# Extra, unread TensorE products behind two token searches and inside a norm, and three weight splits moved from GpSimd to VectorE

## The chip, the core and the metric

The kernel runs on one core of one Trainium2 chip. TensorE (PE) multiplies matrices, VectorE (DVE), ScalarE (ACT) and GpSimd (POOL) work elementwise, SyncE (SP) issues the transfers (DMA). Each engine has its own queue and works through it in order; engines meet at semaphores. The metric is the device time of one execution, in microseconds (us).

## What is computed

Two blocks run one behind the other over 512 tokens of 1024 features. The second has two layers, and what matters lies there: each layer ends with a mixture of 16 experts in which every expert chooses its 64 best tokens, and layer 1 begins with a norm. Cut from the reference:

```python
def modulate_2(x, g, shift, scale):
    return rmsnorm(x, g) * (1 + scale) + shift

def ec_moe(h, w_router, w_gate, w_up, w_down):
    b, n, d = h.shape
    cap = EC_CAPACITY_FACTOR * n // N_EXPERTS            # 64
    aff = jax.nn.softmax(h.astype(jnp.float32) @ w_router.astype(jnp.float32), axis=-1)
    g, idx = lax.top_k(aff.swapaxes(1, 2), cap)
    xs = jax.vmap(lambda hb, ib: hb[ib])(h, idx)
    a = jax.nn.silu(jnp.einsum('becd,edf->becf', xs, w_gate)) * jnp.einsum('becd,edf->becf', xs, w_up)
    y = jnp.einsum('becf,efd->becd', a, w_down) * g[..., None].astype(h.dtype)
    ...

    for l in range(DEPTH_2):                             # second_block, 2 layers
        h = modulate_2(x, norm_mix[l], sh_m, sc_m)
        ...                                              # layer 0: attention, layer 1: odd_mixer
        x = x + g_m * y
        x = x + g_f * ec_moe(modulate_2(x, norm_ffn[l], sh_f, sc_f), ...)
```

## The kernel before

X holds the residual with features on partitions (8 tiles f of 128 features, 512 tokens). Dense products are made in three passes, with each operand split into a high and a low part (`mm3`, line 453): `pieces` (line 437) takes a weight page, copies the high part `wh` on ScalarE (L447) and subtracts it for the low part `wl` (L448), on VectorE as a rule.

**The experts.** `moe` runs 8 rounds of two experts. Each round gathers the chosen tokens (`gather_part`, L1427: the normed tokens `xn` times a one-hot matrix `o`), and then multiplies with the gate, up and down weights (`product`, L1473), 24 MB a round, as transfers fill the buffers that TensorE gives free.

**The search.** `route_half` (line 1275) works on one half of the tokens. After the scores it copies them to `at` (L1307) and runs 8 rounds of `max`, `match_replace` and `max_index` on VectorE (L1314 to L1317). The second half (t0 = 256) runs last; what the first half found is merged with it in `best`. Between the two come `token_major` (line 1374), 32 transposes of X on TensorE (L1386) whose 8 banks ScalarE copies to `xn` (L1390), in layer 1 to `xt` also (L1393). The gather needs both `best` and all of `xn`.

**The norm of layer 1.** `down_last` ends layer 0's last round. It adds the experts' output to X for the first 256 tokens (`combine`, L1534 and L1537), calls `layer1_norm` (line 1593) for them, and does the same for the second 256. `norm_mod` sums the squares (L356, L344), takes the inverse root in small VectorE steps (`rsqrt`, L380 to L382), spreads it over partitions (`spread`, L397), and `norm_apply` makes 8 tiles of normed input (L432, L408, L409). Then the first product of the layer runs over the two halves of the tokens (`dense_f`, 192 products of 256 columns; each result is copied by L1611). Its four weight splits go to GpSimd (`lo`).

The order on each engine comes from a scheduler in the framework: an instruction goes into its engine's queue when the model takes it to be ready, and the queue then is fixed.

```python
        if t0 == 0:
            self.pcs = self.pieces(self.cw, 0, nc.gpsimd)
            self.cw = [next(self.pcs) for _ in range(3)]
```

## Time and profile before

| what | us |
|---|---|
| median of 3 runs | 2106.47 |
| lowest and highest run | 2102.52, 2106.98 |
| profiled execution, whole | 2108.61 |
| its span | 2106.8 |
| TensorE busy | 2003.3 (95%) |
| VectorE busy | 1007.3 (48%) |
| ScalarE busy | 559.0 (27%) |
| GpSimd busy | 17.2 (1%) |

The span is cut into 40 slices of 52.7 us on the profile's page. Transfers run at about 421 GB/s in slices 19 to 24 and 32 to 38, in the expert rounds of the two layers, and far below in most others. [...]

### The profile page before, as it was taken

What the parts mean: (1) busy time and instruction counts of PE and PEld (TensorE: products, weight loads), DVE (VectorE), ACT (ScalarE), POOL (GpSimd) and SP (SyncE); (2) the same over time, 40 slices, a digit from 0 to 9 for tenths busy, and PEclk for the clock granted to TensorE, in tenths of its full rate; (3) what the DMA queues carried; (4) which work ended last, traced back from release to release, by engine and by line L of the source; (5) the groups of instructions that cost most, each with busy time, mean ns of one, the idle gap of its engine ahead of it and who ended that gap; (6) DMA issues with size and microseconds to landing.
All of it is one profiled execution on the core that took longest, in us unless ns stands there. A gap on an engine that the chain in (4) does not pass through costs nothing. (4 is left out here: it accounts for less than half of the span.)

```text
span 2106.8 us, 26895 instructions
## 1 busy us (share of the span) xinstructions
PE 2003.3 (95%) x10922; PEld 1341.0 (64%) x10922; DVE 1007.3 (48%) x2004; ACT 559.0 (27%) x1039; POOL 17.2 (1%) x20
## 2 busy tenths in 40 slices
PE   7999999999999989989999999979998999999997
PEld 5759888788888978865444434428887544444442
DVE  4888995887584569661222212225457122222221
ACT  3344624243343359620000000023234000000000
POOL 0000000000000000000000000010000000000000
PEclk9999999999999999989999999989999999999999
DMA  9826484688411254449999999992254899999998
GB/s 362 288 80 231 172 296 160 222 289 244 144 48 41 79 159 114 174 160 374 408 421 421 421 421 421 420 363 81 100 193 161 328 409 422 422 422 422 422 422 327
DMA packets 158955, 582.84 MB, mean 277 GB/s; under 512 B 12593, under 2 KB 21713, under 8 KB 111984
## 3 DMA queue, kind: packets, MB, share of 16 engines
q1 hardware_dynamic: 158352, 580.70, 72.1%
q8 instruction: 86, 1.41, 0.3%
q10 hardware_dynamic: 288, 0.39, 0.1%
q14 instruction: 37, 0.30, 0.0%
q0 software_dynamic: 192, 0.03, 0.0%
HBM read 571.50 MB, written 2.11 MB: 272 GB/s over the span
## 5 line engine op out<-in xcount | busy, mean ns | idle before, releaser
L453 PE MATMUL mm<-b,wh 128*128 128x512 f32 (+1 forms) x2272 | 578.4, 344 | 1.3 <-ACT b L408 0.9
L453 PEld LDWEIGHTS mm<-b,wh 128*128 128x128 f32 x2272 | 394.9, 191 | 61.5 <-issue 6.7
L453 PE MATMUL mm<-b,wl 128*128 128x512 f32 (+1 forms) x1136 | 388.9, 344 | 0.8 <-DVE wl L448 0.8
L1473 PE MATMUL mm<-w,xs 128*64 128x512 f32 x1152 | 262.8, 600 | 12.6 <-DMA w<-w_u 12.6
L448 DVE TENSOR_TENSOR wl<-w,wh 128x1024 fp32r<-128x1024 f32 x160 | 194.0, 1222 | 160.6 <-ACT wh L447 159.4
L447 ACT CAST wh<-w 128x1024 fp32r<-128x1024 f32 x164 | 170.4, 1049 | 316.9 <-PE mm L453 276.3
L453 PEld LDWEIGHTS mm<-b,wl 128*128 128x128 f32 x1136 | 216.2, 191 | 27.9 <-issue 2.5
L1491 DVE TENSOR_TENSOR ea<-mm,ea 128x512 f32<-128x512 f32 x32 | 22.1, 692 | 398.0 <-PE mm L1473 374.6
L1473 PEld LDWEIGHTS mm<-w,xs 128*64 128x64 f32 x1152 | 84.9, 138 | 175.2 <-issue 141.4
L249 DVE SCALAR_TENSOR_TENSOR w<-w,sc 128x512 f32<-128x512 f32 x252 | 184.6, 748 | 3.8
L453 PE MATMUL mm<-wh,b 128*128 128x512 f32 (+1 forms) x640 | 179.1, 363 | 1.0 <-ACT b L408 1.0
L1473 PE MATMUL mm<-b,xs 128*64 128x512 f32 x720 | 166.1, 594 | 4.6 <-DMA b<-w_u 4.5
L1427 PEld LDWEIGHTS sm<-o,b 128*128 128x128 f32 x1024 | 118.9, 194 | 35.1 <-DVE o L1416 16.4
L1427 PE MATMUL sm<-o,b 128*128 128x128 f32 x1024 | 126.4, 281 | 14.2 <-DVE o L1416 14.2
L453 PEld LDWEIGHTS mm<-wh,b 128*128 128x128 f32 x640 | 114.5, 190 | 24.4 <-issue 5.0
L1473 PEld LDWEIGHTS mm<-b,xs 128*64 128x64 f32 x720 | 57.8, 137 | 104.4 <-issue 83.2
L453 PE MATMUL mm<-wl,b 128*128 128x512 f32 (+1 forms) x320 | 115.6, 361 | 0.0
L1473 PE MATMUL mm<-w,eaT 128*64 128x512 f32 x512 | 112.6, 594 | 2.1 <-ACT eaT L1504 2.1
L1487 ACT ACTIVATE ea<-mm 128x512 f32<-128x512 f32 x32 | 19.1, 597 | 321.0 <-PE mm L1473 321.0
L1504 ACT COPY eaT<-mm 128x512 f32<-128x512 f32 x32 | 17.2, 589 | 304.1 <-PE mm L1503 303.8
L1431 DVE TENSOR_SCALAR xs<-sm,fgs 128x128 f32<-128x128 f32 x128 | 44.3, 405 | 109.9 <-PE sm L1427 109.9
L1473 PEld LDWEIGHTS mm<-w,eaT 128*64 128x64 f32 x512 | 36.2, 137 | 72.4 <-issue 68.4
(333 smaller groups left out, 2158.5 us busy)
## 6 DMA issues: line engine op xcount, KB each, us to landing
w<-w_g SPq DMA_DIRECT2D x80, 1024.0 KB, 19.7
w<-w_d SPq DMA_DIRECT2D x64, 1024.0 KB, 18.4
w<-w_u SPq DMA_DIRECT2D x64, 1024.0 KB, 19.7
b<-w_u SPq DMA_DIRECT2D x50, 1024.0 KB, 19.8
w<-ada_w SPq DMA_DIRECT2D x48, 1024.0 KB, 5.3
b<-w_g SPq DMA_DIRECT2D x40, 1024.0 KB, 19.8
b<-w_d SPq DMA_DIRECT2D x40, 1024.0 KB, 19.8
w<-w SPq DMA_DIRECT2D x32, 1024.0 KB, 7.0
```

The lines of the kernel that those rows point to most:

```text
L249: nc.vector.scalar_tensor_tensor(acc, w[:, i], sc, acc, op0=ALU.mult, op1=ALU.add)
L447: self.nc.scalar.copy(vh, w[:, i:i + kp])
L448: (lo or self.nc.vector).tensor_tensor(vl, w[:, i:i + kp], vh.bitcast(F32), op=ALU.subtract)
L453: mm = lambda *v, **k: self.pe(self.nc.tensor.matmul(*v, **k))
L1427: self.pe(nc.tensor.matmul(ps[:, 128 * i:128 * i + 128], self.xn[:, t, 128 * k:128 * k + 128], o[:, t], start=(t == 0), stop=(t == 3), ski ...
L1431: nc.vector.tensor_scalar(xs[:, k], ps[:, 128 * i:128 * i + 128], self.fgs[:, 0, k:k + 1], self.fgs[:, 1, k:k + 1], op0=ALU.mult, op1=ALU.add)
L1473: self.pe(self.nc.tensor.matmul(ps[n][64 * b:64 * b + 64], lhs[:, k, 64 * b:64 * b + 64], w[b][k % 2][:, 512 * n:512 * n + 512], start=(k ...
L1487: nc.scalar.activation(av[:, :, 64 * n:64 * n + 64], gp[n].rearrange("p (q k) -> p k q", k=KT), AF.Silu)
L1491: nc.vector.tensor_tensor(av[:, :, c], up[n].rearrange("p (q k) -> p k q", k=KT), av[:, :, c], op=ALU.mult)
L1504: nc.scalar.copy(aT[:, 4 * h:4 * h + 4], ps.rearrange("p (k n) -> p k n", k=4))
```

## The change

Three things are added or moved:

- `warm` (new) is a TensorE product whose result nobody reads. In the second half's search four of them run, each with 8 of the found maxima (rounds 3 to 6) as weights and 512 columns of `iota`.
- In layer 1's norm of the first 256 tokens, two such products of 256 columns follow the sums of squares, and two of 512 columns follow the spread.
- The splits of the layer's first weights go from GpSimd to VectorE, and are called at tiles 0, 3 and 6 of `norm_apply`, with their place in VectorE's order pinned.

```diff
+        if warm:
+            for t in range(2):
+                self.warm(s[:, 128 * t:128 * t + 128], 256)
...
+    def warm(self, by, n, ps=None):
+
+        ps = self.mm_ps() if ps is None else ps
+        self.nc.tensor.matmul(ps[:by.shape[1], :n], by, self.iota[:by.shape[0], :n], start=True, stop=True,
+                              skip_group_check=True)
+        return ps
...
+        warm = amid is not None and t0 == 0
+        r = self.rsqrt(self.sumsq(xs, t0, n, None, warm), n // 128)
+        rep = self.spread(r, n // 128)
+        if warm:
+            for i in range(2):
+                self.warm(r[:, i:i + 1].to_broadcast([128, 32]), 512)
+        self.norm_apply(xs, t0, n, rep, g, sh, xh, xl, amid)
...
         for f in range(KT):
+            if amid:
+                amid(f)
...
-                (lo or self.nc.vector).tensor_tensor(vl, w[:, i:i + kp], vh.bitcast(F32), op=ALU.subtract)
+                ins = self.nc.vector.tensor_tensor(vl, w[:, i:i + kp], vh.bitcast(F32), op=ALU.subtract)
+                if pinned:
+                    self.tc.keep_in_program_order(ins)
...
             nc.vector.max_index(ix[:, c], g[:, 0, c], cur)
+            if t0 and 3 <= i < 7:
+                wp = self.warm(g[:, 0, c], 512, None if i == 3 else wp)
...
+        amid = None
         if t0 == 0:
-            self.pcs = self.pieces(self.cw, 0, nc.gpsimd)
-            self.cw = [next(self.pcs) for _ in range(3)]
-        else:
+            self.pcs = self.pieces(self.cw, 0, True)
+            self.cw = []
+            amid = lambda f: self.cw.append(next(self.pcs)) if f in (0, 3, 6) else None
+        self.norm_mod(self.X, t0, n, self.g1, self.mods["shm1"], *self.x1, amid)
+        if t0:
             self.cw += self.pcs
```

The queues show where these land. TensorE behind layer 1's search, before (`gt` are the maxima of the first half, `gc` a copy of them, `X` the input of the transposes, `o` and `xs` the gather, `w` an expert's weights; layer 0 has the same rows without `m_gf`):

```order
L1305 MATMUL mm<-cs,af 16x128 x2
L1324 MATMUL mm<-cs,gt 64x16 x2
L1386 MATMUL mm<-cs,X 128x128 x6
L1329 MATMUL mm<-cs,gc 16x64 x2
L1386 MATMUL mm<-cs,X 128x128 x26
L397 MATMUL mm<-cs,m_gf_417 128x128 x8
L1413 MATMUL sm<-best,cs 128x64 x2
L1427 MATMUL sm<-o,b_12234 128x128 x4
L1401 MATMUL sm<-cs,best 64x8 x4
L1473 MATMUL mm<-w,xs 64x512 x4
L1427 MATMUL sm<-o,b_12234 128x128 x7
L1473 MATMUL mm<-w,xs 64x512 x4
```

The same place in the changed kernel:

```order
L1324 MATMUL mm<-cs,af 16x128 x2
L417 MATMUL mm<-iota,gt 8x512 x4
L1345 MATMUL mm<-cs,gt 64x16 x2
L1407 MATMUL mm<-cs,X 128x128 x4
L1350 MATMUL mm<-cs,gc 16x64 x2
L1407 MATMUL mm<-cs,X 128x128 x28
L400 MATMUL mm<-cs,m_gf_417 128x128 x8
L1434 MATMUL sm<-best,cs 128x64 x2
L1448 MATMUL sm<-o,b_12252 128x128 x3
L1422 MATMUL sm<-cs,best 64x8 x4
L1448 MATMUL sm<-o,b_12252 128x128 x5
L1494 MATMUL mm<-w,xs 64x512 x8
```

The four unread products (L417) stand ahead of all 32 transposes, where before the transposes came right behind the scores' own.

TensorE in layer 1's norm of the first 256 tokens, before (`oT`, `yh`, `yl` are the combine, `sq` and `sqs` the squares, `rs` the inverse root, `b` the normed input):

```order
L1534 MATMUL mm<-oT,yh 128x256 x5
L1534 MATMUL mm<-oT,yl 128x256 x5
L1534 MATMUL mm<-oT,yh 128x256
L1534 MATMUL mm<-oT,yl 128x256
L1534 MATMUL mm<-oT,yh 128x256
L1534 MATMUL mm<-oT,yl 128x256
L1534 MATMUL mm<-oT,yh 128x256
L1534 MATMUL mm<-oT,yl 128x256
L356 MATMUL sm<-sq,cs 32x256 x4
L344 MATMUL sm<-cs,sqs 128x1 x2
L397 MATMUL sm<-cs,rs 128x128 x2
L356 MATMUL sm<-sq,cs 32x256 x4
```

The same place in the changed kernel:

```order
L1555 MATMUL mm<-oT,yh 128x256 x4
L1555 MATMUL mm<-oT,yl 128x256 x4
L359 MATMUL sm<-sq,cs 32x256 x4
L344 MATMUL sm<-cs,sqs 128x1 x2
L417 MATMUL mm<-iota,sqs 128x256 x2
L400 MATMUL sm<-cs,rs 128x128 x2
L417 MATMUL mm<-iota,rs 32x512 x2
L1555 MATMUL mm<-oT,yh 128x256
L1555 MATMUL mm<-oT,yl 128x256
```

The combine of the second 256 tokens (four pairs, of which the first stands in the last two rows) has moved behind the spread and the unread products; then come the second half's squares and the first product of the layer.

VectorE at the same place in the changed kernel, from the inverse root on (before, the rows with `wl` and with `X<-mm` are not there: the four `X<-mm` ran ahead of the root):

```order
L385 SCALAR_TENSOR_TENSOR rs<-rs 128x2
L465 TENSOR_TENSOR wl<-w,wh 128x1024
L449 SCALAR_TENSOR_TENSOR nt<-X,g_m_8435,sm 128x256
L412 SCALAR_TENSOR_TENSOR b_10479<-nt,m_shm_413,b_10478 128x256
L1558 SCALAR_TENSOR_TENSOR X<-mm,m_gf_411,X 128x256
L449 SCALAR_TENSOR_TENSOR nt<-X,g_m_8435,sm 128x256 x2
L1558 SCALAR_TENSOR_TENSOR X<-mm,m_gf_411,X 128x256 x2
L412 SCALAR_TENSOR_TENSOR b_10479<-nt,m_shm_413,b_10478 128x256 x2
L465 TENSOR_TENSOR wl<-w,wh 128x1024
```

Its end lies behind the second half's last tile:

```order
L449 SCALAR_TENSOR_TENSOR nt<-X,g_m_8435,sm 128x256 x2
L412 SCALAR_TENSOR_TENSOR b_10479<-nt,m_shm_413,b_10478 128x256 x2
L465 TENSOR_TENSOR wl<-w,wh 128x1024 x8
L1639 TENSOR_TENSOR w<-mm,w 128x512 x2
```

The first of these eight `wl` is the fourth split of the first weights, which GpSimd made before; 72 of the 192 products stand behind it in TensorE's queue.

## Rows read from the trace of the kernel before

**Rows 1.** Chain of waits, layer 1: start us, us, engine, line, instructions.

```profile
1431.09 4.29 PE mm L453 x35
...
1812.55 3.63 PE mm L1473 x16
1816.58 16.61 DMA w<-w_u
```

**Rows 2.** Windows: length, busy PE, PEld, DVE, ACT, POOL; clock, DMA share, GB/s.

```profile
1638.00:1640.00 2.00, 2.00 (x9) 0.57 (x6) 0.19 (x1) 0.00 (x0) 0.00 (x0) 0.78 0.00 0
...
1705.00:1710.00 5.00, 5.00 (x26) 1.72 (x24) 0.00 (x0) 0.00 (x0) 0.00 (x0) 1.00 0.83 295
```

**Rows 3.** Timeline, norm and search: start, us, engine, line, tiles [idle before].

```profile
1414.83 6.95 POOL L448 TENSOR_TENSOR wl<-w,wh 128x1024 fp32r<-128x1024 f32 x3 [0.97 <-ACT wh L447]
...
1417.23 2.27 DVE L381 TENSOR_TENSOR rs<-rs 128x2 f32<-128x2 f32 x1
...
1419.54 2.26 DVE L382 SCALAR_TENSOR_TENSOR rs<-rs 128x2 f32<-128x2 f32 x1
...
923.90 0.16 DVE L381 TENSOR_TENSOR rs<-rs 128x2 f32<-128x2 f32 x1
```

**Rows 4.** Timeline, from the norm's first product to its block's last copy.

```profile
1424.97 1.44 PE L453 MATMUL mm<-b,wh 128*128 128x256 f32 x5 [0.88 <-ACT b L408]
...
1454.01 0.37 ACT L1611 COPY w<-mm 128x256 f32<-128x256 f32 x1
```

**Rows 5.** Windows as before: layer 0's last expert, the norm, layer 0's transposes.

```profile
1388.00:1390.00 2.00, 2.00 (x6) 0.50 (x6) 0.00 (x0) 0.16 (x1) 0.00 (x0) 0.50 1.04 384
...
1428.00:1430.00 2.00, 2.00 (x13) 1.19 (x10) 1.02 (x3) 0.00 (x0) 0.00 (x0) 0.50 0.00 0
...
932.00:934.00 2.00, 1.77 (x15) 1.53 (x13) 1.93 (x10) 1.85 (x4) 0.00 (x0) 0.92 0.86 348
```

**Rows 6.** Timeline, VectorE in and after the norm's second half.

```profile
1436.92 0.89 DVE L409 SCALAR_TENSOR_TENSOR b<-nt,m_shm,b 128x256 fp32r<-128x256 f32 x2 [0.19 <-ACT b L408]
...
1451.30 4.63 DVE L448 TENSOR_TENSOR wl<-w,wh 128x1024 fp32r<-128x1024 f32 x4 [7.72 <-ACT wh L447]
```

**Rows 7.** Timeline, a weight load of products of 512 columns.

```profile
1388.64 0.24 PEld L1568 LDWEIGHTS mm<-w,eaT 128*64 128x64 f32 x2 [0.61 <-issue]
```

**Rows 8.** Timeline, VectorE in the two searches: copy of the scores, two maxima.

```profile
926.79 0.41 DVE L1307 COPY at<-mm 16x256 f32<-16x256 f32 x1 [0.77 <-PE mm L1305]
...
1621.33 0.41 DVE L1307 COPY at<-mm 16x256 f32<-16x256 f32 x1 [0.77 <-PE mm L1305]
...
1629.83 0.40 DVE L1314 MAX8 gt<-at 16x8 f32<-16x256 f32 x1
...
1631.07 0.40 DVE L1314 MAX8 gt<-at 16x8 f32<-16x256 f32 x1
```

**Rows 9.** Timeline, TensorE from layer 0's transposes to its first gate products.

```profile
929.23 4.54 PE L1386 MATMUL mm<-cs,X 128*128 128x128 f32 x26
938.08 0.66 PE L1413 MATMUL sm<-best,cs 128*128 128x64 f32 x4 [4.31 <-DVE best L1340]
939.52 2.08 PE L1427 MATMUL sm<-o,b 128*128 128x128 f32 x8 [0.78 <-DVE o L1416]
...
942.10 3.68 PE L1473 MATMUL mm<-w,xs 128*64 128x512 f32 x8
```

**Rows 10.** Timeline, ScalarE's copies of the transposes, layer 0, then layer 1.

```profile
932.50 2.42 ACT L1390 ACTIVATE b<-mm,rs 128x512 f32<-128x512 f32 x4 [0.15 <-PE mm L1386]
...
1625.54 0.70 ACT L1390 ACTIVATE b<-mm,rs 128x512 f32<-128x512 f32 x1
...
1630.78 0.80 ACT L1390 ACTIVATE b<-mm,rs 128x512 f32<-128x512 f32 x1
```

**Rows 11.** Timeline, TensorE in layer 1's first gather and gate products.

```profile
1643.42 2.05 PE L1427 MATMUL sm<-o,b 128*128 128x128 f32 x16
1645.40 3.65 PE L1473 MATMUL mm<-w,xs 128*64 128x512 f32 x16
```

## The prediction, made before the changed kernel had run

> **What bounds the kernel now.** I read the 40 slices first: the two expert stages run at the speed of the transfers, the stretches between them at that of TensorE. Then the chain of waits: through layer 1's dense stage it is TensorE alone, and in the expert stage TensorE holds it until 1816, where the chain passes to transfers and stays with them nearly to the end [rows 1]. Then the windows: behind the search the transfers stand still [rows 2] (first row), since every buffer is full and TensorE has not begun to free them; as late as 1705 to 1710 their share is 0.83 [rows 2], because a buffer came free late. From there on they are full, and the bytes left are fixed. So a microsecond that TensorE gains or loses up to about 1709 moves the end by one; what it gains later is worth nothing. Layer 0 has the same form. The timelines of the searches and of the norm then give the terms. All of this is the profiled execution, of 2108.6 us (span 2106.8); the median of the runs is 2106.5, 2.1 less. I add my sum to the median. About 0.2%, 4.2 us, is what a measurement of this kernel can tell from no change.

> **The norm, splits.** GpSimd's splits run while VectorE makes the inverse root: two steps on 128x2 values took 2.27 and 2.26 us [rows 3], against 0.16 for the same line elsewhere [rows 3] (last row). Without GpSimd the root ends at 1417.23 + 2 x 0.2 = 1417.6 rather than at 1421.8: 4.2 us earlier. That is not the gain, for three things now stand between the root and the first useful product, which began at 1424.97 [rows 4].

> **The norm, TensorE.** [...] Behind the unread ones stands the moved combine, 8 products at 0.123 (4.29 us for 35 [rows 1]) or twice that: 1.0 or 2.0; four square sums, 0.4 or 0.85; and the spread itself, 0.5 or 1.0 (four of the eight steps of 2.08 us, [rows 9]). All at half clock, the first useful product starts at 1417.6 + 1.0 + 3.4 + 2.0 + 0.9 = 1424.9, as before; all at full clock at 1421.2. TensorE rests before the root here as it did before, so I expect 0.50 at first and a rise within this dense stretch, as within the 26 transposes of [rows 9], where the window from 932 has 0.92 [rows 5]. I take 1424. From there it runs at full clock, where before it had 0.50 in [rows 5] (second row) until about 1431.

> **The norm, VectorE.** Now VectorE is what comes last. Its third step after the root adds the first moved combine to X and waits for TensorE until about 1422.9. Behind it stand 30 tile steps at 0.445 ([rows 6], 0.89 for two), three splits at 1.16 (4.63 for four), four additions at 0.445, small steps of 1.0, and eight waits for ScalarE of 0.19 [rows 6]: 13.4 + 3.5 + 1.8 + 1.0 + 1.5 = 21.2. So the fourth split ends at 1444.1, and 72 products behind it take 72 x 0.123 = 8.9: the block ends at 1453.0. Before, its last copy began at 1454.01 [rows 4]. The term is -1.0. Its ends: all at full clock gives 1450.4, -3.6; a second fall of the clock while TensorE waits for the fourth split would cost what the half clock cost from 1424.97 to 1431.09, 3.1, and gives +2.0.

> **The search, order.** Before, the transposes filled the search, and TensorE then rested 4.31 us for `best` [rows 9]. In the changed queue the four products come first, and each waits for its maximum. A round takes 1.24 [rows 8]; the fourth maximum ends 0.45 + 3 x 1.24 + 0.40 = 4.6 after the copy begins, in layer 0 at 926.79 + 4.6 = 931.35, in layer 1 at 1621.33 + 4.6 = 1625.9. Until then TensorE rests, so it starts at half clock. All four at half clock end 6.84 later (938.3, 1632.8); if the clock rises after two, the seventh maximum and two at full clock set the end (936.5, 1631.1). I take the middle, W = 937.4 and 1631.9. The search itself ends earlier, at 936.8 (the eighth maximum and one index step). Queued behind the four products stand the merge's small products, all 32 transposes and so ScalarE's copies, on which the gather waits.

> Layer 0: small products 0.6, a first bank of transposes 0.45 (4 of the 26 in 4.54 us at half clock for most of it, [rows 9]), then eight banks paced by the transposes and by ScalarE at 0.6 a bank (2.42 for four, [rows 10]): `xn` is whole at W + 6.3, the first gather done at W + 6.6 = 944.0. Before, it was done at 939.52 + 2.08 = 941.6 [rows 9]: +2.4. Then the clock gives back: the first eight gate steps took 3.68 [rows 9] and take 3.65 / 2 = 1.83 at full clock [rows 11]: -1.85. Layer 0: **+0.6**, from -0.3 to +1.5.

> Layer 1: ScalarE makes two copies of each bank there, (1630.78 - 1625.54) / 5 = 1.05 a bank [rows 10]. `xn` is whole at W + 1.05 + 7 x 1.05 + 0.7 = W + 9.1 = 1641.0, the first gather at 1641.3. Four more gather products (1.03), eight gate products (3.65) and three gather products (0.77) follow, and at 1646.75 TensorE has done what it had done at 1643.42 before [rows 11]: **+3.3**, from 2.4 to 4.2. X is free for the next weights only after the transposes, some 9 us later than before, but the transfers stood still then [rows 2] (first row), so that costs nothing; without that rest it would delay the weights by up to that much.

> **Nothing else.** Eight small router products move forward within TensorE's busy stretch. Two transfers of layer 1 change places in SP's queue, and two weight pages wait for VectorE's fourth split rather than GpSimd's; all land tens of microseconds before they are used, behind the dense products of [rows 1], and would cost their lateness beyond that.

> **Sum.** 0.6 - 1.0 + 3.3 = +2.9, from -1.5 to +7.7: **2109.4 us** by the median, 2111.5 by the profiled execution's own time.

> **A rule against it.** While only transposes ran, the clock rose: TensorE did nothing but the 26 transposes from 929.23 on [rows 9], and the window from 932 has 0.92 [rows 5]. [...] The row speaks against the rule; of that rival's chance I give it 0.03.

> **The rivals.** First, **the low clock stays** through the four products, whose weights have only 16 rows and 8 columns. Then W is 938.3 and 1632.8, the transposes begin at twice their price, `xn` comes some 1.7 us later in layer 0 and 0.6 in layer 1, so +3.2 and +4.8, with the norm +7.0: 2113.5. For it: no row shows so narrow a product. Against it: they keep TensorE as densely busy as the transposes of [rows 9], under which the clock rose. It decides from where the first transpose runs at 0.25 rather than 0.12. Second, **the norm keeps its clock**: the unread products of 256 columns fill enough of the wait, the term is -3.6, the sum +0.3: 2106.8. [...] Third, **the search does what the change says**: the transposes are done before the four products begin, and the clock holds through the gather. Then each layer gains half of 2.08 and 1.85, 2.9 together, and the sum is -5.8 - 1.0 = -6.8: 2099.7. Against it: the queue's order, and TensorE took its queue in order at every wait I read.

> **How the numbers follow.** Forecast 0.62, low clock 0.13, norm at full clock 0.15, search as meant 0.10. The forecast's own spread passes +4.2 in some 0.19 of its 0.62. Slower by over 0.2%: 0.13 + 0.19 = 0.32; within 0.2%: 0.43 + 0.15 = 0.58; faster: 0.10. The range, 2104 to 2114, takes in the forecast with its ends, the second rival and the first; the third is left out.

> **What would show it.** Right: after the search's fourth maximum four L417 products, then all transposes, the gather starting near 944 and 1641; VectorE's two root steps at 0.16; a short wait of TensorE for the fourth split near 1444. Wrong: transposes ahead of L417; clock 0.50 at the first gather; the first dense product before 1422; a transfer, not TensorE, that holds layer 1's first gate products.

## The result, and the profile after

The changed kernel takes 2116.36 us (median of 6 runs, 2113.64 to 2121.62) beside 2103.1 of the kernel before (median of 6); the ratio is 1.0054, 95% interval 1.0039 to 1.0068: 11.4 us longer (8.2 to 14.3; the two medians lie 13.3 apart). Forecast were +2.9, and a range of 2104 to 2114, which ended at +7.5. The profiled execution has a span of 2115.0.

Single executions of one kernel differ by several us, and the stages say where: the time up to layer 0's scores lies between 921.8 and 929.7 and layer 0's expert stage between 452.5 and 455.8 in the traces below, whatever the kernel. I therefore compare three stretches, each between two TensorE records of the timeline. A **search** runs from the start of the scores' two products (L1305 before, L1324 after) to the end of the 32nd gate or up record from the weight pages; the **norm** stretch from the first combine product of 256 columns (L1534, L1555) to layer 1's scores. Before: 28.91, 210.20 and 28.35. After: 32.67, 209.21 and 35.98, that is +3.76, -0.99 and +7.63, in sum +10.4. From there to the end the two traces take the same: 457.8 before, 457.7 after.

TensorE in layer 0's search, timeline of the changed kernel, beside [rows 9] (start, us, engine, line, tiles [idle before]):

```profile
924.06 0.58 PE L1324 MATMUL mm<-cs,af 128*16 128x128 f32 x2 [3.22 <-DVE af L1319]
929.32 6.99 PE L417 MATMUL mm<-iota,gt 16*8 16x512 f32 x8 [4.67 <-DVE gt L1333]
936.23 0.60 PE L1345 MATMUL mm<-cs,gt 16*64 16x16 f32 x4
936.77 1.11 PE L1407 MATMUL mm<-cs,X 128*128 128x128 f32 x4
...
938.35 4.42 PE L1407 MATMUL mm<-cs,X 128*128 128x128 f32 x28
942.61 0.56 PE L1434 MATMUL sm<-best,cs 128*128 128x64 f32 x4
943.95 1.16 PE L1448 MATMUL sm<-o,b 128*128 128x128 f32 x8 [0.78 <-DVE o L1437]
...
945.61 1.94 PE L1494 MATMUL mm<-w,xs 128*64 128x512 f32 x8 [0.17 <-DVE xs L1452]
```

TensorE rests 4.67 us for the fourth maximum, the four products (eight records) take 6.99, and behind them everything stands in one row: transposes, the spread of `best`, 0.78 of waiting for the one-hot rows, the gather. The gather and the first gate products, 1.16 and 1.94, run at a clock of 1.00 (windows from 942, 944 and 946), where [rows 9] has 2.08 and 3.68.

The same place in layer 1, in the chain of waits (start, us, engine, line, instructions), which answers to [rows 1]:

```profile
1626.55 6.99 PE mm L417 x8
1633.54 0.53 PE mm L1345 x4
...
1635.65 5.57 PE mm L1407 x28
1641.22 1.79 PE mm L400 x16
1643.01 0.41 PE sm L1434 x4
1643.44 0.70 DVE o L1437
1644.19 0.94 PE sm L1448 x6
```

The unread products are the longest piece of the chain up to the gather. Behind the transposes the chain passes through 16 records of the gate's broadcasts (L400), which before ran while TensorE had nothing else to do.

The clock, by the windows view (stretch, length, busy time of PE, PEld, DVE, ACT, POOL, then granted clock, where 1.00 is full speed, DMA share, GB/s), which answers to [rows 5] and [rows 2]:

```profile
932.00:934.00 2.00, 2.00 (x4) 0.26 (x2) 1.97 (x9) 0.00 (x0) 0.00 (x0) 0.50 0.00 0
...
938.00:940.00 2.00, 2.00 (x12) 1.80 (x11) 0.84 (x4) 1.11 (x2) 0.00 (x0) 0.50 0.00 0
940.00:942.00 2.00, 2.00 (x17) 2.00 (x16) 0.00 (x0) 1.81 (x4) 0.00 (x0) 0.81 0.00 0
942.00:944.00 2.00, 1.22 (x13) 1.08 (x10) 0.69 (x1) 2.00 (x4) 0.00 (x0) 1.00 0.00 0
...
1638.00:1640.00 2.00, 2.00 (x11) 2.00 (x10) 0.00 (x0) 2.00 (x5) 0.00 (x0) 0.50 0.00 0
...
1713.00:1718.00 5.00, 5.00 (x27) 1.59 (x24) 0.00 (x0) 0.00 (x0) 0.00 (x0) 1.00 0.82 298
```

TensorE is without a gap from 929.32 on, and the clock is 0.50 through all four products and on into the transposes; only there it rises. The last row is the dip of the transfers of [rows 2] (0.83 at 1705), now 8 us later. Layer 1's search ends 8.2 us later than before (1657.28 beside 1649.05), and so does the whole span (2115.0 beside 2106.8): TensorE's start moves the end one for one, as forecast.

The norm, timeline of the changed kernel, beside [rows 3], [rows 4] and [rows 6], and one window:

```profile
1419.24 0.16 DVE L384 TENSOR_TENSOR rs<-rs 128x2 f32<-128x2 f32 x1
1419.43 0.16 DVE L385 SCALAR_TENSOR_TENSOR rs<-rs 128x2 f32<-128x2 f32 x1
...
1420.82 2.48 PE L417 MATMUL mm<-iota,rs 128*32 128x512 f32 x4
...
1424.95 0.50 PE L472 MATMUL mm<-b,wh 128*128 128x256 f32 x2
...
1444.61 1.22 DVE L465 TENSOR_TENSOR wl<-w,wh 128x1024 fp32r<-128x1024 f32 x1
...
1445.88 0.39 PE L472 MATMUL mm<-b,wl 128*128 128x256 f32 x1 [0.78 <-DVE wl L465]
```

The combine starts 1.59 later than before (1412.09 beside 1410.50), so the first dense product, at 1424.95, comes 1.6 earlier against it; the root's steps are down to 0.16; and TensorE waits 0.78 for the fourth split.

### The profile page after: what moved, and what is told of

It reads as the page before. It is cut to its first block, busy times and chain, and to the rows that moved or that the text cites. A ratio compares the mean times of both kernels' runs of the same rounds, so it can differ in the third digit from the quotient of the medians.

```text
span 2115.0 us, 26936 instructions
## 1 busy us (share of the span) xinstructions
PE 2014.5 (95%) x10946; PEld 1342.0 (63%) x10946; DVE 1007.8 (48%) x2008; ACT 558.9 (26%) x1039; POOL 7.8 (0%) x16
## 5 line engine op out<-in xcount | busy, mean ns | idle before, releaser
L465 DVE TENSOR_TENSOR wl<-w,wh 128x1024 fp32r<-128x1024 f32 x164 | 198.8, 1220 | 164.3 <-ACT wh L464 163.3
```

Of the source, the lines that this page charges most:

```text
L465: ins = self.nc.vector.tensor_tensor(vl, w[:, i:i + kp], vh.bitcast(F32), op=ALU.subtract)
```

## Experiments

The table has the three stretches of each profiled execution, their sum against the kernel before, and the ratio of the runs. A stretch is one execution's; two kernels ran only once and have no ratio. All ratios lie within 1% of 1; a difference is called one here when the interval leaves out 1.

| kernel | layer 0 search | norm | layer 1 search | sum, us | ratio (95%) |
|---|---|---|---|---|---|
| before | 28.91 | 210.20 | 28.35 | 0 | 1 |
| changed | 32.67 | 209.21 | 35.98 | +10.4 | 1.0054 (1.0039 to 1.0068) |
| e1_search_only | 32.97 | 210.31 | 35.52 | +11.3 | 1.0054 (1.0034 to 1.0074) |
| e2_norm_only | 28.69 | 208.73 | 28.68 | -1.4 | 1.0001 (0.9986 to 1.0017) |
| e3_wide | 30.04 | 209.24 | 31.63 | +3.5 | 1.0019 (1.0004 to 1.0035) |
| e4_cols | 34.07 | 208.21 | 36.02 | +10.8 | one run |
| e5_rows | 29.24 | 209.27 | 31.61 | +2.7 | one run |
| e6_two | 29.24 | 208.77 | 32.36 | +2.9 | 1.0022 (1.0005 to 1.0039) |
| e7_behind | 26.07 | 208.73 | 27.01 | -5.6 | 0.9978 (0.9967 to 0.9989) |
| e8_behind_narrow | 28.86 | 208.27 | 29.12 | -1.2 | 1.0002 (0.9993 to 1.0012) |
| e9_three | 26.06 | 209.32 | 26.07 | -6.0 | 0.9969 (0.9959 to 0.998) |
| e10_norm_two | 26.07 | 211.10 | 26.36 | -3.9 | 0.9991 (0.9982 to 1.0) |
| e11_norm_none | 26.07 | 209.38 | 26.07 | -5.9 | 0.9958 (0.9944 to 0.9973) |
| e12_split_early | 26.05 | 207.01 | 26.06 | -8.3 | 0.9965 (0.9954 to 0.9977) |

My first theory, A, read off the trace of after: the searches are the whole loss, by the queue and the clock. Its rival, B: the searches cost what was forecast, and the norm or the transfers the rest.

### One part alone

The kernel before, with this alone and the helper `warm` (e1_search_only):

```diff
             nc.vector.max_index(ix[:, c], g[:, 0, c], cur)
+            if t0 and 3 <= i < 7:
+                wp = self.warm(g[:, 0, c], 512, None if i == 3 else wp)
```

> The kernel before, with the four unread products in each search and nothing else of the change. Theory A (the loss is all in the searches: the four products stand ahead of the transposes, run at half clock to their end, and the one-hot chain and layer 1's gate broadcasts then follow in a row): 3.8 us in layer 0 and 7.6 in layer 1, +11.4, 1.0054. Theory B (the searches cost what was forecast, and the rest of the loss comes from the norm or from transfers that shift): +3.9, 1.0019.

And the changed kernel without these two lines (e2_norm_only):

> The changed kernel without the four products in the searches: only layer 1's norm is changed, and the search's order is that of before. Theory A: -1.0 us, 0.9995, the last copy of the norm's block some 1.0 earlier than before against the start of the combine. Theory B: it carries the rest of the loss, +7, 1.0035.

Measured: 1.0054 and 1.0001. The searches alone lose 11.4 us, as much as the whole change, and the norm alone doesn't carry the +7 of theory B. Its -1.4 by the stretches lies inside the interval of the runs (-2.9 to +3.6), which cannot show a gain of that size. B is out.

### Two products instead of four

The changed kernel with this edit (e6_two):

```diff
-            if t0 and 3 <= i < 7:
+            if t0 and 3 <= i < 5:
```

> The changed kernel with two unread products in each search (behind the fourth and fifth maximum) instead of four. Theory A (queued work ahead of the transposes, one for one): two products of 1.71 us at half clock less in each layer, 6.8 in all: +4.5, 1.0021. Theory S (the search's last maxima and the merge hold the gather, not the queue): under 2 us less, 1.0045 or more.

Measured: 1.0022. The searches are 3.43 and 3.62 shorter than the changed kernel's, beside 3.5 for two of the four products (half of 6.99). What stands ahead of the transposes costs one for one; neither VectorE's last maxima nor the merge takes the place of what is removed.

### What keeps the clock down

Theory N: the narrow weights do. Theory K: not the weights, but the rest before. The changed kernel with wide weights (e3_wide):

```diff
-        g = self.sml.tile([NE, 2, CAP], F32, name="gt", tag="gt")
+        gg = self.sml.tile([128, 2, CAP], F32, name="gt", tag="gt")
+        if t0:
+            nc.gpsimd.memset(gg, 0.0)
+        g = gg[:NE]
...
-                wp = self.warm(g[:, 0, c], 512, None if i == 3 else wp)
+                wp = self.warm(gg[:, 0, 8 * i:8 * i + 1].to_broadcast([128, 128]), 512, None if i == 3 else wp)
```

> The changed kernel, with weights of 128 rows and 128 columns for the searches' four products (a column of the maxima repeated, rows from 16 on zero) instead of 16 rows and 8 columns; same columns streamed, same place, same waits. Theory N (narrow weights keep the clock down): the clock rises while the four run; layer 0's last of them ends near 935 instead of 936.2 against the same start, layer 1's near 1631.7 instead of 1633.5, the transposes start at full clock; 4 us less than the changed kernel, +7, 1.0033. Theory K (the kind or width of weights doesn't matter, the engine rested too long before): 0.50 until well into the transposes, as in the changed kernel, 1.0054.

The other two take one size each: `g[:, 0, 8 * i:8 * i + 1].to_broadcast([16, 128])` for 128 columns (e4_cols), `gg[:, 0, c]` for 128 rows (e5_rows). The streamed operand, `iota`, always has as many rows as the weights; its rows hold numbers, while the weights' rows from 16 on are zero.

> The changed kernel with weights of 16 rows and 128 columns for the searches' four products, for one look at the clock. If the columns of the weights decide, the clock rises while the four run, as with 128 rows and 128 columns (the eight records of them take 6.2 us in layer 0, 5.4 in layer 1); if the rows decide, 0.50 to their end and 6.99.

> The changed kernel with weights of 128 rows and 8 columns for the searches' four products, for one look at the clock. If the rows of the weights decide, the clock rises while the four run (under 6.5 us for the eight records in layer 0); if the columns decide, 0.50 to their end and 6.99.

The four products of layer 0, and the first transposes behind them, in the timeline of the kernel with wide weights:

```profile
929.41 6.22 PE L417 MATMUL mm<-iota,gt 128*128 128x512 f32 x8 [4.83 <-DVE gt L1336]
...
935.89 0.66 PE L1410 MATMUL mm<-cs,X 128*128 128x128 f32 x4
```

In the timeline of the kernel with 16 rows and 128 columns:

```profile
930.31 7.19 PE L417 MATMUL mm<-iota,gt 16*128 16x512 f32 x8 [4.67 <-DVE gt L1333]
```

In the timeline of the kernel with 128 rows and 8 columns:

```profile
929.23 5.41 PE L417 MATMUL mm<-iota,gt 128*8 128x512 f32 x8 [4.83 <-DVE gt L1336]
```

A window of the kernel with 16 rows and 128 columns (the clock stands behind POOL's column):

```profile
934.00:936.00 2.00, 2.00 (x4) 0.88 (x3) 1.87 (x8) 0.00 (x0) 0.00 (x0) 0.50 0.00 0
```

Two windows of the kernel with 128 rows and 8 columns:

```profile
932.00:934.00 2.00, 2.00 (x4) 0.32 (x3) 1.97 (x9) 0.00 (x0) 0.00 (x0) 0.77 0.00 0
934.00:936.00 2.00, 2.00 (x16) 1.13 (x15) 0.96 (x6) 0.40 (x1) 0.00 (x0) 1.00 0.00 0
```

The streamed columns, the place and the busy time are the same, and the rest before is 4.67 or 4.83; with 16 rows the clock stays at 0.50 to the end, with 128 rows it rises while the four run, and the columns of the weights do not decide. Layer 1 of the two kernels that ran once says the same: 7.19 us for the four with 16 rows and 128 columns, 5.39 with 128 rows and 8 columns. N holds, as a matter of rows; K is out. Between 16 and 128 rows nothing was run. Wide weights make the searches 2.6 and 4.4 shorter than the changed kernel's, 7.0 in sum, where I had expected 4: the transposes behind also run at full clock (the first four took 0.66 instead of 1.11). The 4.4 that the wide kernel still loses in its searches (1.1 and 3.3) I put down to the place, which the next kernel changes.

### Behind the transposes

The products leave the loop and stand in the second half's merge, which is written behind the transposes (e7_behind):

```diff
+        wp = None
+        for i in range(4, 8):
+            wp = self.warm(gg[:, 0, 8 * i:8 * i + 1].to_broadcast([128, 128]), 512, wp)
         m = self.sml.tile([NE, CAP], U32, name="smask", tag="smask", bufs=1)
```

> The changed kernel with the searches' four products written behind the transposes (so that they wait for the last four maxima in the rest that TensorE had there) and with weights of 128 rows and 128 columns. Theory O (place and width are the fault): nothing useful stands behind them but the chain to the gather, they fill 3.4 of the rest of 4.3 us in layer 0 and all of the 3.2 in layer 1, the clock is 1.00 at the first gather and gate products: half of 0.66 + 2.08 + 0.60 + 3.68 in layer 0 and of 1.11 + 2.08 + 0.60 + 2.83 in layer 1 comes back, less what is bound by columns, 5.6 us, and 1.0 from the norm: -6.6 against the kernel before, 0.9969. Theory D (the last product delays the chain, or the clock falls all the same): between -1 and +2, 0.9995 to 1.001.

With `g[:, 0, 8 * i:8 * i + 8]`, the change's narrow weights, at the same place (e8_behind_narrow):

> As the kernel with the four products behind the transposes, but with the change's own weights of 16 rows and 8 columns. Theory N (narrow products don't hold the clock): it falls behind the transposes as in the kernel before, the first gather runs at 0.50, and only the norm's 1.0 is gained: 0.9995, or worse by what a product at half clock delays the chain. Theory K (any work holds it): as with wide weights, -6.6, 0.9969.

Layer 0's search in the timeline of the kernel with wide weights:

```profile
928.00 4.75 PE L1411 MATMUL mm<-cs,X 128*128 128x128 f32 x26
932.59 4.29 PE L417 MATMUL mm<-iota,gt 128*128 128x512 f32 x8
...
938.22 1.16 PE L1452 MATMUL sm<-o,b 128*128 128x128 f32 x8 [0.78 <-DVE o L1441]
```

The same in the timeline of the kernel with narrow weights:

```profile
932.73 1.94 PE L417 MATMUL mm<-iota,gt 16*8 16x512 f32 x4
934.88 1.02 PE L417 MATMUL mm<-iota,gt 16*8 16x512 f32 x2 [0.22 <-DVE gt L1333]
...
938.59 2.07 PE L1449 MATMUL sm<-o,b 128*128 128x128 f32 x8 [0.78 <-DVE o L1438]
```

And one window of layer 1 of the kernel with narrow weights:

```profile
1628.00:1630.00 2.00, 2.00 (x11) 2.00 (x11) 0.00 (x0) 0.59 (x1) 0.00 (x0) 0.50 0.98 406
```

Wide: 0.9978, faster than before, theory O; both gathers are at full clock (1.16 us for eight records each). In layer 1 the gain is half of layer 0's (1.34 beside 2.84): the products alternate there with the gate's broadcasts, and together they push the spread of `best` 1.0 later. Narrow: 1.0002, theory N, and layer 0's gather takes 2.07 as before. In layer 1 the clock is down at 1628 although TensorE has had no rest since 1615.4: it fell behind narrow products, with two of the gate's broadcast records (0.49 us) between each and the next and no gap. At the same place among the same broadcasts, wide products kept it up (1.00 in e7_behind's windows from 1624 and 1626): the first gather begins 14.2 behind the scores there, with narrow products 16.3. Of three products in layer 1 I then expected the missing 1.0 (`lr` is the layer; e9_three):

```diff
-        for i in range(4, 8):
+        for i in range(4, 7 if self.lr else 8):
```

> The kernel with four wide products behind the transposes, with three instead of four in layer 1, where the eight gate broadcasts fill part of the rest too. Theory Q (in layer 1 the fourth product delayed the one-hot chain): best's spread begins 1.0 us earlier against the scores' products, the clock still holds: search of layer 1 26.0 instead of 27.0, 1.0 us less than with four, about 0.997 of before. Theory C (three don't hold the clock): the gather of layer 1 runs at 0.50 again, its search takes 28.3 as before.

Measured: layer 1's search 26.07, 0.94 shorter, the clock holds (1.16 us for the first eight gather records); 0.9969.

### The norm

Nine kernels of the table (the changed one and the eight from e2 to e9) have the changed norm with all four unread products; their stretches lie between 208.2 and 209.3, those of the two with the norm of before at 210.2 and 210.3. A single norm stretch is thus good to about 1 us.

On top of e9_three, without the two products of 512 columns behind the spread (e10_norm_two):

```diff
-        if warm:
-            for i in range(2):
-                self.warm(r[:, i:i + 1].to_broadcast([128, 32]), 512)
```

> As the kernel with four and three wide products behind the transposes, and in layer 1's norm without the two products of 512 columns behind the spread; the two of 256 before the root stay. Theory P (they are work in the way, 2.0 to 2.5 us of it): from the combine of the norm's second half to layer 1's scores 0.5 to 1.5 us less than in the kernel with them (208.2 to 209.3). Theory H (they hold the clock): the first dense products run at 0.50, and the stretch is as long as before, 210.2.

Measured: 211.10, 0.9 longer than before, and by the runs 0.9991 beside 0.9969 with them. P is out. H had the half clock of the first dense products right, but not the rest: without these products the moved combine goes ahead of the spread in TensorE's queue, TensorE waits twice, and the clock that had risen falls again. Timeline of this kernel:

```profile
1416.21 0.71 PE L400 MATMUL sm<-cs,rs 128*128 128x128 f32 x4 [1.04 <-DVE rs L385]
...
1418.99 1.44 PE L469 MATMUL mm<-b,wh 128*128 128x256 f32 x5 [1.50 <-ACT b L411]
```

And two of its windows:

```profile
1416.00:1418.00 2.00, 1.28 (x12) 0.68 (x12) 2.00 (x4) 0.54 (x3) 0.00 (x0) 1.00 0.00 0
...
1420.00:1422.00 2.00, 2.00 (x13) 0.97 (x13) 0.92 (x3) 0.91 (x2) 0.00 (x0) 0.50 0.04 8
```

Without the two before the root as well (`self.warm(s[:, 128 * t:128 * t + 128], 256)`), so that only the splits are VectorE's (e11_norm_none):

> As the kernel with four and three wide products behind the transposes, and in layer 1's norm no unread product at all: only the splits are VectorE's, the combine of both halves stands ahead of the root again. Theory P (the splits alone are the gain, and the unread products with the moved combine give most of it back): the root ends 4.2 us earlier, the first dense product begins near 10.3 us behind the start of the combine instead of 14.5 (before) and 12.9 (changed kernel), at half clock for some 3 us: the stretch from the combine to layer 1's scores takes 206 to 207 instead of 210.2; with the searches 8 to 9 us less than before, 0.996. Theory H (the unread products carry the gain): 210 or more, and 0.998.

The first dense product comes 10.38 behind the combine's start (1414.22 beside 1403.84), as theory P had it, but the stretch takes 209.38 and not 206 to 207: about what the kernels with all four unread products take (208.2 to 209.3; 209.32 in e9_three, from which this one differs in the norm alone). The lead goes at half clock (0.50 in its windows from 1414, 1416 and 1418) and in two waits. VectorE in the timeline of this kernel:

```profile
1427.79 0.87 DVE L443 SCALAR_TENSOR_TENSOR nt<-X,g_m,sm 128x256 f32<-128x256 f32 x2 [3.33 <-PE sm L397]
```

TensorE in the same timeline:

```profile
1437.79 0.39 PE L466 MATMUL mm<-b,wl 128*128 128x256 f32 x1 [1.03 <-DVE wl L459]
```

VectorE waits 3.33 for the spread of the second half, which has its fixed place behind the first half's products in TensorE's queue, and TensorE 1.03 for the fourth split. So P is right that the splits alone earn a gain like that of the whole norm, and wrong on what the unread products cost: no gain or loss by all four shows beyond the 1 us by which such stretches differ. By the runs it is 0.9958, which the intervals do not tell from 0.9969. Last, the fourth split is made among the first half's tiles (e12_split_early):

```diff
-            amid = lambda f: self.cw.append(next(self.pcs)) if f in (0, 3, 6) else None
+            amid = lambda f: self.cw.append(next(self.pcs)) if f in (0, 2, 4, 6) else None
```

> As the kernel with wide products behind the transposes and no unread product in the norm, with the fourth split before the first half's fifth tile's successors (tiles 0, 2, 4, 6) instead of behind the second half. Theory W (TensorE's wait for the fourth split is the norm's last loss): the wait of 1.0 us near 33 us behind the start of the combine is gone, and the stretch from there to layer 1's scores takes 208.3 instead of 209.4, 0.9953 of before. Theory V (VectorE is the bound whatever the order): the second half's tiles come 1.2 us later, TensorE waits there instead, 209.4 again.

TensorE has no such wait any more, and the stretch takes 207.01, 2.4 less where W expected 1.1. W's wait is gone, and V is out; where the other 1.3 comes from is not shown (the router's bias products also went back behind the block, as before, and a wait of 0.33 behind them went too). The runs, 0.9965, do not tell it from the two others. These three kernels (0.9969, 0.9958, 0.9965) are faster than the kernel before; by the stretches the last one is the best, 8.3 us under the kernel before.

## Why the prediction was wrong

**Which place decides** held: in the two traces TensorE's later start of layer 1's experts moved the end by 8.2 us, one for one, and what follows the search takes the same (457.8 and 457.7).

**The norm** held: -1.0 forecast, -0.99 measured; with -0.9 to -2.0 over the nine kernels that have this norm, so close a match is chance. VectorE came last, its fourth split ended at 1445.83, 1444.24 against before's combine (forecast 1444.1), the first dense product at 1423.4 (forecast 1424). No run shows the 3.4 us that the sum for TensorE takes for the two unread products of 512 columns: they took 2.48, at 0.50 in the window from 1420 and 1.00 in that from 1422. Not forecast were a second fall of the clock near 1439 and that the unread products have no visible part in the gain: the kernel without them has much the same stretch.

**Layer 0's search**, +0.6 forecast, +3.76 measured; two steps failed. W, the end of the four products, was taken in the middle, 11.2 behind the scores' start, between a clock that rises after two of them and one that stays low; it was 12.17 (936.23 beside 924.06), all at half clock: +0.9. No run shows the 6.84 us that it takes for four products at half clock: the changed kernel's four took 6.99; and where the clock was 1.00, in e8_behind_narrow's window from 932, two took 1.94. And "the first gather done at W + 6.6", 0.3 behind `xn`: it was done at W + 8.9 (945.11), +2.3, since it did not follow `xn` but the spread of `best`, the one-hot rows and the whole gather, which come in a row behind the last transpose (W + 6.4): 0.56, 0.78 and 1.16. I had let the gather follow `xn`, as if that chain were done by then. In the kernel before, the transposes had ended before `best` came, so that only `best` counted; in the changed kernel `best` is there at 939.43, and the spread waits for TensorE. The rows of the order had shown it behind the transposes. The term for `xn` was wrong as well, without being what came last: its pieces add up to W + 5.9 where W + 6.3 is written, and ScalarE's last copy ended at 944.06, W + 7.8. The clock gave back what was forecast: 3.68 to 1.94. In sum 0.6 + 0.9 + 2.3 = 3.8.

ScalarE's last copies in the timeline of the changed kernel, layer 0, then layer 1:

```profile
940.35 3.71 ACT L1411 ACTIVATE b<-mm,rs 128x512 f32<-128x512 f32 x6 [0.17 <-PE mm L1407]
...
1643.01 0.79 ACT L1411 ACTIVATE b<-mm,rs 128x512 f32<-128x512 f32 x1
```

**Layer 1's search**, +3.3 forecast, +7.63 measured: the same two steps. W came 12.16 behind the scores instead of 11.2, +1.0, with the four at 6.99 again where 6.84 was taken. `xn` was whole at W + 10.3 (1643.80) instead of W + 9.1, and again it was not what came last: behind the transposes, which end at W + 7.6, stand 1.79 of gate broadcasts, 0.56 of spread, 0.78 of one-hot rows and a first gather with the slots in its midst. It is done near W + 12.8, where the forecast said W + 9.4, +3.4. The prediction let the broadcasts out altogether; they were in the quoted order, and in before they were free, since TensorE rested anyway (3.25 us behind them). In sum 3.3 + 1.0 + 3.4 = 7.7.

**The rivals.** The first one, low clock through the narrow products, is what happened: 0.50 until the transposes, and 1.11 for the first four of them, against 0.66 at full clock in the kernel with wide weights. Its 2113.5 was short because it left out the same pieces of the chain. The argument against it was wrong: that products which keep TensorE as busy as the transposes would lift the clock as they did. The second rival (full clock in the norm) and the third (transposes ahead) did not happen in the changed kernel; the third's gain was there to be had: 5.1 us in the searches (2.85 and 2.28) with the products behind the transposes and on all rows.

**The transposes and the clock.** As in the kernel before ([rows 9], [rows 5]), the clock rose while transposes ran: the narrow products had not lifted it in 6.99 us, and within the transposes that follow it went from 0.50 in the window from 938 to 0.81 in that from 940 and 1.00 in that from 942.

## What to carry to other kernels

An unread product is work in an in-order queue: it is free only where nothing that will be waited for stands behind it, so put it behind the last useful work before the wait, and list all that follows it in the queue up to the next product that counts. Here two products fewer ahead of the transposes made the searches 3.43 and 3.62 us shorter; behind them, four wide ones in layer 0 left the spread of `best` at 11.84 us behind the scores, where it stood at 11.91 without any, and in layer 1 the four pushed it 1.0 later. Make it as tall as a real product: here products on 16 rows left the clock where rest had left it before (the first gather of layer 0 took 2.07 and 2.08 us). And ask of each filler whether the kernel without it is any slower; in this norm, moving the splits away from GpSimd alone gave about as much as the splits and the fillers together (209.38 and 209.32, 210.20 before).
